# First layer's modulation vectors as column-tiled fp32 products, tokens loaded first, GpSimd's two-operand arithmetic on VectorE

## The chip, the core and the metric

One core of one Trainium2 chip runs the whole program. The time is device microseconds of one launch, the median of several runs. A core has TensorE (matmuls; PE in the rows, and PEld for its weight loads), VectorE (DVE), ScalarE (ACT), GpSimd (POOL) and SyncE (SP), whose queue issues the DMAs of this kernel.

## The reference, cut to what matters

Two layers work on 256 latent and 256 context tokens of 1024 channels. Each layer has a token-mixing part and a SwiGLU part, and each part is framed by norms that are modulated by six vectors made from the conditioning vector:

```python
silu_c = jax.nn.silu(c); silu_cc = jax.nn.silu(c_ctx)[None]
for l in range(DEPTH):                                   # DEPTH = 2
    mod_x = (silu_c @ w_ada[l] + b_ada[l]).reshape(B, 1, 6, D)
    mod_c = (silu_cc @ w_ada[l] + b_ada[l]).reshape(1, 1, 6, D)
    h = modulate(rms_norm(x, g_pre_mix[l]), mod_x[:, :, 0], mod_x[:, :, 1])
    hc = modulate(rms_norm(ctx, g_pre_mix[l]), mod_c[:, :, 0], mod_c[:, :, 1])
    ...   # p = h @ w_in[l]; attention, pooling and recurrent branch, gates, w_out -> mix_l
    x = x + mod_x[:, :, 2] * rms_norm(mix_l, g_post_mix[l])
    x = ffn_sublayer(x, mod_x[:, :, 3], mod_x[:, :, 4], mod_x[:, :, 5], ...)
    ...   # the same for ctx, in the first layer only
```

So each layer needs a shift, a scale and a gate (m = 0, 1, 2) for the mixing and three more (m = 3, 4, 5) for the SwiGLU part, for two streams in the first layer: w_ada[l] is 1024 x 6144, 25 MB a layer, read for two rows of products (one per stream).

## The kernel before, in words

All four token tiles of 128 (two of context, then two of latent tokens) stand in the moving operand, 512 columns. Weights are loaded as 512 KB pieces (`load_w`, line 605) and split into a high part (fp32r, a cast on ScalarE or VectorE) and a low part (a subtraction; `split_w`, line 614); activations are split likewise (`hilo`, line 640). Each product is then three fp32r matmuls: high x high, high x low, low x high (`mm3`, line 628). In the rows `whi`, `wlo` are the parts of weights, `hh`, `hl` those of the modulated tokens; `pm` and `pa` are the two sets of four PSUM banks.

Nothing is written to an engine directly. A `Queue` records every operation, and `Program.schedule` (line 256) is a list planner: it knows a price for each operation (`price`, line 207), the buffers, the PSUM banks and the port that VectorE and GpSimd share (`shares_port`, line 198), and hands the operations out in order of readiness and priority. An operation recorded through `either` or `also` may go to either of two engines, whichever is free first in the plan; so some of the two-operand subtractions (`wlo` above all) land on GpSimd. The order on each engine is fixed by that plan; on the chip the engines only wait for each other's semaphores. All records have one line, 409, so the rows are told apart by tiles.

**Start** (`start`, line 1177). The first layer's shift and scale are made on TensorE in eight blocks of 128 channels. A block is loaded as four DMAs of 256 KB (`start_load`), split into parts by casts and subtractions, and multiplied with the four columns of `cT` (high and low part of the two conditioning vectors): 16 fp32r matmuls of 256 columns a block. Two fp32 column pieces per block turn the rows back into columns. After every second block the tokens' transposes are modulated (`h_pair`, line 738) and multiplied with 512 columns of w_in (`products`), for the recurrent branch. The loads of the tokens stand between the first blocks' on SP's queue.

**Jobs.** All other modulation vectors are jobs that advance by one step at each `tick` (line 669), which the gemm loops call. A step loads 256 KB of w_ada into one of three `ra` buffers and VectorE multiplies it by a column of the silu and adds it to `acc`, 128 x 512 (`ada_acc`, line 651; one multiply-add per stream). After eight steps `ada_columns` (line 686) transposes `acc` on TensorE and sums it on VectorE into columns; `ada_gate` (line 700) sums it over the partitions with a `partition_all_reduce` on GpSimd and multiplies it by the post-norm's gain. The first layer's mixing runs the six jobs of m = 3, 4, 2; its SwiGLU part the job pairs of its own m = 5 and of all of the second layer's.

**Order of the stages**, in us of the profile: start to 68; the pooling, gate and q, k, v products to 190; recurrent chains, attention and the merges of the three branches to 395 (`rnn_chain`, `attention`, `merge`); output projection and norms to 510; SwiGLU to 815, norms to 861; the second layer's mixing to 1050, its norms to 1116, its SwiGLU to the end.

## Time and profile before

| | |
|---|---|
| median of 3 runs | 1312.26 us (1311.13 to 1313.22) |
| the profiled execution | 1311.86 us, span 1310.1 us, mean granted clock 0.984 |
| TensorE busy | 1238.5 us, 95% of the span |
| VectorE busy | 966.5 us, 74% |
| ScalarE busy | 631.1 us, 48% |
| GpSimd busy | 276.5 us, 21% |
| DMA | 199.5 MB, 152 GB/s over the span |

The span runs from the first instruction of the program to its last; the profiled time holds what lies around it as well. A busy TensorE counts the pipelined length of its matmuls, so what a matmul costs in a stream is the distance of two starts, which is shorter than the mean duration of a record. The granted clock is a share of the full 2.4 GHz.

### The profile page before, as it was taken

Reading aid. Unit: us, or ns where it says so; the run is one execution under the profiler, and the core shown is the slowest. Engines: PE = TensorE matmul, PEld = TensorE weight load, DVE = VectorE, ACT = ScalarE, POOL = GpSimd, SP = SyncE. Lnnn points to the kernel's source line nnn. Section 1 sums busy time; section 2 is a strip of 40 time slices with the busy share of each in tenths; the row PEclk is TensorE's granted clock in tenths of the full one; section 3 lists DMA queues with packets and bytes.
Section 4 is the critical chain, followed back from the end, with each engine's and each line's share of the span. In section 5 each row is a group of like instructions: output and inputs, shape, how many; then the busy total and the mean of one; then the engine's idle time right before and its main releaser. Section 6 shows DMA issues by size and latency. Waiting matters only on the chain.

```text
span 1310.1 us, 19123 instructions
## 1 busy us (share of the span) xinstructions
PE 1238.5 (95%) x7003; PEld 1067.9 (82%) x7003; DVE 966.5 (74%) x1552; ACT 631.1 (48%) x1173; POOL 276.5 (21%) x242
## 2 busy tenths in 40 slices
PE   6999998999999999999999999999888897999998
PEld 4888876777878887888888887799787796999986
DVE  5799989889788575688377731879998876555564
ACT  7736577477733373222122222666786744544400
POOL 4322023252541243010001004312333402000000
PEclk9999999999999999999999999999998999999999
DMA  9753523533238453656567831444344255566662
GB/s 292 241 143 91 160 89 107 166 114 89 60 97 265 154 173 90 200 171 199 177 210 225 251 114 62 137 118 141 113 129 130 81 168 166 149 179 191 181 193 78
DMA packets 249797, 199.53 MB, mean 152 GB/s; under 512 B 12724, under 2 KB 214740, under 8 KB 249704
## 3 DMA queue, kind: packets, MB, share of 16 engines
q1 hardware_dynamic: 249704, 198.32, 50.2%
q8 instruction: 55, 0.90, 0.3%
q14 instruction: 38, 0.31, 0.1%
HBM read 195.14 MB, written 3.15 MB: 151 GB/s over the span
## 4 chain that ended last, share of the span: by engine, by line
PE 77%; DVE 10%; ACT 5%; POOL 3%; issue 3%; DMA 1%; SPq 0%; DVEq 0%; POOLq 0%; ACTq 0%
PE pm L409 62%; PE pa L409 15%; DVE t L409 5%; ACT t L409 2%; POOL s L409 2%; DVE b L409 1%; DVE acc L409 1%; ACT junk_a L409 1%; DVE wlo L409 1%; POOL wlo L409 1%; ACT whi L409 1%; DVE s L409 1%; ACT b L409 1%; POOL b L409 0%; DMA raw<-in_w_in_dram 0%
## 5 line engine op out<-in xcount | busy, mean ns | idle before, releaser
L409 PE MATMUL pm<-hh,wlo 128*128 128x256 f32 (+1 forms) x1472 | 487.9, 333 | 9.9 <-DVE wlo L409 8.2
L409 PE MATMUL pm<-hl,whi 128*128 128x256 f32 (+1 forms) x1472 | 487.1, 332 | 3.4 <-DVE hl L409 3.4
L409 PE MATMUL pm<-hh,whi 128*128 128x256 f32 (+1 forms) x1472 | 485.3, 334 | 3.1 <-ACT hh L409 2.7
L409 ACT ACTIVATE whi<-raw 128x1024 fp32r<-128x1024 f32 (+1 forms) x225 | 229.4, 1026 | 265.6 <-PE pm L409 149.4
L409 DVE TENSOR_TENSOR wlo<-raw,whi 128x1024 fp32r<-128x1024 f32 (+1 forms) x212 | 254.2, 1202 | 96.7 <-ACT whi L409 92.7
L409 PEld LDWEIGHTS pm<-hh,wlo 128*128 128x128 f32 x1472 | 282.2, 192 | 37.2 <-DVE wlo L409 9.5
L409 PEld LDWEIGHTS pm<-hl,whi 128*128 128x128 f32 x1472 | 282.3, 192 | 29.1 <-DVE hl L409 4.5
L409 PEld LDWEIGHTS pm<-hh,whi 128*128 128x128 f32 x1472 | 280.0, 192 | 29.9 <-ACT hh L409 4.1
L409 POOL TENSOR_TENSOR wlo<-raw,whi 128x1024 fp32r<-128x1024 f32 (+1 forms) x58 | 142.3, 2458 | 316.9 <-ACT whi L409 143.4
L409 DVE SCALAR_TENSOR_TENSOR acc<-ra,csilu,acc 128x512 f32<-128x512 f32 x224 | 172.6, 795 | 28.2 <-DMA ra<-in_w_ada_dram 26.8
L409 PE MATMUL pm<-whi,b 128*128 128x512 f32 x360 | 140.7, 391 | 0.0
L409 PE MATMUL pa<-whi,b 128*128 128x512 f32 x360 | 140.4, 390 | 0.0
L409 PE MATMUL pm<-b,whi 128*128 128x512 f32 (+1 forms) x384 | 101.0, 344 | 13.6 <-ACT b L409 13.6
L409 ACT ACTIVATE tm<-pm 128x512 f32<-128x512 f32 (+1 forms) x92 | 44.7, 487 | 113.1 <-PE pm L409 112.8
L409 PEld LDWEIGHTS pm<-b,whi 128*128 128x128 f32 x384 | 66.7, 192 | 22.1 <-ACT b L409 14.4
L409 PEld LDWEIGHTS pm<-whi,b 128*128 128x128 f32 x360 | 67.6, 188 | 13.8
L409 PEld LDWEIGHTS pa<-whi,b 128*128 128x128 f32 x360 | 67.6, 188 | 13.8
L409 POOL PARTITION_ALL_REDUCE b<-acc x12 | 41.0, 3440 | 172.0 <-DVE acc L409 79.8
L409 PE MATMUL pm<-wlo,b 128*128 128x512 f32 x180 | 70.2, 390 | 3.1 <-DVE wlo L409 3.1
L409 POOL TENSOR_SCALAR s<-s 128x1 f32<-128x1 f32 x26 | 9.9, 382 | 298.1 <-ACT junk_a L409 297.6
L409 PE MATMUL pa<-wlo,b 128*128 128x512 f32 x180 | 70.4, 391 | 0.0
L409 PE MATMUL pm<-b,wlo 128*128 128x512 f32 (+1 forms) x192 | 65.5, 342 | 1.3 <-POOL wlo L409 1.3
(169 smaller groups left out, 1539.5 us busy)
## 6 DMA issues: line engine op xcount, KB each, us to landing
raw<-in_w_gu_dram SPq DMA_DIRECT2D x88, 512.0 KB
raw<-in_w_in_dram SPq DMA_DIRECT2D x84, 512.0 KB
ra<-in_w_ada_dram SPq DMA_DIRECT2D x160, 256.0 KB
raw<-in_w_down_dram SPq DMA_DIRECT2D x44, 512.0 KB
b<-in_w_ada_dram SPq DMA_DIRECT2D x32, 256.0 KB
raw<-in_w_out_dram SPq DMA_DIRECT2D x16, 512.0 KB
raw<-in_w_pool_o_dram SPq DMA_DIRECT2D x8, 512.0 KB
raw<-in_w_rnn_o_dram SPq DMA_DIRECT2D x8, 512.0 KB
```

Source lines behind the costliest of these rows:

```text
L409: op.fn(*op.args, **op.kw)
```

## The change

The modulation vectors of the first layer but for the SwiGLU gate are made by TensorE in full fp32, without a split. The two silu columns, padded with zeros to 32 columns (`cT`), are the weights. Eight blocks of 128 rows of w_ada are the moving operands, 512 columns each, and block k goes to the strip of 32 array columns k % 4 (`tile_position`), so that four sums of two blocks stand in four quarters of one bank. Four column pieces with a summing matrix turn it into columns (start and `row_columns`), or one product with a spread summing matrix broadcasts it to all partitions (`row_gate`), in place of transposes with reductions and of the all-reduce. In the start the four token tiles are loaded ahead of all modulation loads, four blocks of 256 channels (shift and scale) replace eight of 128, and all but the first of the `products` are 512 columns wide instead of two times 256. `either` is gone: the two-operand arithmetic that could go to either engine is VectorE's. The norms' small instructions, the all-reduces of the remaining gate jobs and the memsets stay on GpSimd. `ra` has eight buffers instead of three; a slot of the small working tiles shrinks from 640 to 576 columns; the padding tile moves and grows; the planner's DMA rate and the price of a tiled fp32 matmul are changed.

```diff
-SLOT = 640
+SLOT = 576
+BIAS = 2
...
-    c[:4, C_SUM:C_SUM + 2] = np.tile(np.eye(2, dtype=np.float32), (2, 1))
+    for j in range(4):
+        c[32 * j:32 * j + 2, C_SUM:C_SUM + 2] = np.eye(2, dtype=np.float32)
+    c[BIAS, C_SUM:C_SUM + 2] = 1.0
...
-    DMA_RATE = 360e3
+    DMA_RATE = 320e3
...
-                op.cost = max(n * 1.667e-3, 0.106)
+                op.cost = max(n * 1.667e-3 / (4 if "tile_position" in kw else 1), 0.106)
...
+    BUFS = {"raw": 4, "w": 10, "B": 30, "hT": 16, "t": 13, "s": 24, "ra": 8, "acc": 3, "hx": 3, "tm": 2}
...
-    PAD = 176
-    BUFS = {"raw": 4, "w": 10, "B": 30, "hT": 16, "t": 13, "s": 24, "ra": 3, "acc": 3, "hx": 3, "tm": 2}
+    PAD = 208
...
+        self.spread = self.const([128, 2, 128], F32, "spread")
+        nc.vector.tensor_copy(self.spread, self.c[:, C_SUM:C_SUM + 2].unsqueeze(2).to_broadcast([128, 2, 128]))
...
-        self.cT = self.const([128, 8, 4], F32R, "cT")
-        cst = cs.rearrange("p s k -> p k s")
-        nc.vector.tensor_copy(self.cT[:, :, 0:2], cst)
-        nc.vector.tensor_tensor(out=self.cT[:, :, 2:4], in0=cst, in1=self.cT[:, :, 0:2], op=ALU.subtract)
+        self.cT = self.const([128, 8, 32], F32, "cT")
+        nc.gpsimd.memset(self.cT, 0.0)
+        nc.vector.tensor_copy(self.cT[:, :, 0:2], cs.rearrange("p s k -> p k s"))
...
-        nc.either("tensor_tensor", out=lo[:, 0:n], in0=raw[:, 0:n], in1=hi[:, 0:n], op=ALU.subtract)
+        nc.vector.tensor_tensor(out=lo[:, 0:n], in0=raw[:, 0:n], in1=hi[:, 0:n], op=ALU.subtract)
...
-            r = nc.vector.tensor_tensor(out=lo, in0=src, in1=hi, op=ALU.subtract)
-            if src.tensor.name not in nc.psum:
-                nc.also(r, "gpsimd", "tensor_tensor", out=lo, in0=src, in1=hi, op=ALU.subtract)
+            nc.vector.tensor_tensor(out=lo, in0=src, in1=hi, op=ALU.subtract)
...
+    def ada_rows(self, l, m, h, done):
+        nc, w = self.nc, self.I["w_ada"][l]
+        c0 = m * D + h * 512
+        nc.sync.dma_start(out=self.brow[BIAS:BIAS + 1, :], in_=self.I["b_ada"][l:l + 1, c0:c0 + 512])
+        raws, landings = [], []
+        for k in range(8):
+            raws.append(self.sb("ra", [128, 512], F32, "ra"))
+            landings.append(nc.sync.dma_start(out=raws[k], in_=w[k * 128:(k + 1) * 128, c0:c0 + 512]))
+            if k < 7:
+                yield
+        ps = self.ps("pa")
+        for k in range(8):
+            j = k % 4
+            nc.after = landings
+            nc.tensor.matmul(ps[32 * j:32 * j + 32, :], lhsT=self.cT[:, k, :], rhs=raws[k], start=k < 4, stop=k >= 4,
+                             tile_position=(0, 32 * j))
+            nc.after = []
+        ar = self.sb("acc", [128, 512], F32, "acc")
+        nc.vector.tensor_tensor(out=ar, in0=ps, in1=self.brow, op=ALU.add)
+        done(ar)
+        yield
+    def row_columns(self, l, m, h, mods, g):
+        def done(ar):
+            nc = self.nc
+            dst = mods[m % 3][:, h * 4:(h + 1) * 4, :]
+            pc = self.ps("pa")
+            for i in range(4):
+                nc.tensor.matmul(pc[:, 2 * i:2 * i + 2], lhsT=ar[:, i * 128:(i + 1) * 128], rhs=self.c[:, C_SUM:C_SUM + 2],
+                                 start=True, stop=True)
+            p3 = pc[:, 0:8].rearrange("p (i s) -> p i s", s=2)
+            if m % 3 == 0:
+                nc.vector.tensor_copy(dst, p3)
+            else:
+                nc.vector.scalar_tensor_tensor(out=dst, in0=p3, scalar=1.0, in1=self.col(l, g, h * 4, 4).unsqueeze(2).to_broadcast([128, 4, 2]),
+                                               op0=ALU.add, op1=ALU.mult)
+        return self.ada_rows(l, m, h, done)
+    def row_gate(self, l, m, h, g_post, streams, ggs):
+        def done(ar):
+            nc = self.nc
+            gp = self.T(512)
+            nc.sync.dma_start(out=gp, in_=self.I[g_post][l, h * 512:(h + 1) * 512].partition_broadcast(128))
+            for s in streams:
+                ps = self.ps("pa")
+                nc.tensor.matmul(ps, lhsT=self.spread[:, s], rhs=ar, start=True, stop=True)
+                gg = self.B()
+                nc.vector.tensor_tensor(out=gg, in0=ps, in1=gp, op=ALU.mult)
+                ggs[s, h] = gg
+        return self.ada_rows(l, m, h, done)
...
-        blocks = [self.start_load(0)]
-        self.start_columns()
-        x = {t: self.load_x(t) for t in (0, 1)}
-        blocks.append(self.start_load(1))
-        hT, first = self.start(x, blocks)
+        hT, first = self.start()
+        x = {}
...
+    def start_load(self, c):
+        for k in range(8):
+            raw = self.B()
+            landing = self.nc.sync.dma_start(
+                out=raw.rearrange("p (m c) -> p m c", m=2),
+                in_=self.I["w_ada"][0][k * 128:(k + 1) * 128, 0:2 * D].rearrange("p (m c) -> p m c", m=2)[:, :, c * 256:(c + 1) * 256])
+            raws.append((raw, landing))
         return raws
...
+    def start_mods(self, c, raws, mt):
+        nc = self.nc
+        ps = self.ps("pa")
+        for k in range(8):
+            j = k % 4
+            nc.after = [landing for _, landing in raws[k - j:k - j + 4]]
+            nc.tensor.matmul(ps[32 * j:32 * j + 32, :], lhsT=self.cT[:, k, :], rhs=raws[k][0], start=k < 4, stop=k >= 4,
+                             tile_position=(0, 32 * j))
+            nc.after = []
+        ar = self.sb("tm", [128, TOK], F32, "tm")
+        nc.scalar.activation(ar, ps, AF.Copy)
+        pc = self.ps("pa")
+        for i in range(4):
+            nc.tensor.matmul(pc[:, 2 * i:2 * i + 2], lhsT=ar[:, i * 128:(i + 1) * 128], rhs=self.c[:, C_SUM:C_SUM + 2],
+                             start=True, stop=True)
+        for m in range(2):
+            nc.vector.tensor_tensor(out=mt[:, 2 * c:2 * c + 2, m], in0=pc[:, 4 * m:4 * m + 4].rearrange("p (k s) -> p k s", k=2),
+                                    in1=self.gcol[:, 16 + 8 * m + 2 * c:18 + 8 * m + 2 * c].unsqueeze(2).to_broadcast([128, 2, 2]),
+                                    op=ALU.add)
+        for k in (2 * c, 2 * c + 1):
+            nc.vector.tensor_scalar(out=mt[:, k, 1], in0=mt[:, k, 1], scalar1=1.0, scalar2=self.col(0, "g_pre_mix", k),
+                                    op0=ALU.add, op1=ALU.mult)
+    def start(self):
+        nc = self.nc
+        x = {t: self.load_x(t) for t in range(4)}
         mt = self.const([128, 8, 2, 2], F32, "mods0")
         mods = (mt[:, :, 0], mt[:, :, 1])
         hT = [None] * 8
         rx = [self.ps() for _ in range(4)]
+        raws = self.start_load(0)
+        self.start_columns()
+        xn = [self.pre_norm(x[t]) for t in range(4)]
...
+            parts = [slice(0, 256), slice(256, TOK)] if kp == 0 else [slice(0, TOK)]
+            for sl in parts:
...
+        ws = {}
+        for kp in range(5):
+            if kp < 4:
+                self.start_mods(kp, raws, mt)
+                raw = self.load_rx(kp)
+                if kp < 3:
+                    raws = self.start_load(kp + 1)
+                if kp == 2:
+                    self.load_rows()
+                    self.load_tables()
                 for s in range(2):
-                    self.h_pair(k // 2, s, [xn[2 * s], xn[2 * s + 1]], mods, hT)
-                if k > 1:
-                    products(k // 2 - 1, w)
-                w = self.split_w(raw)
-        products(3, w)
+                    self.h_pair(kp, s, xn[2 * s:2 * s + 2], mods, hT)
+                ws[kp] = self.split_w(raw)
+            if kp > 0:
+                products(kp - 1, ws.pop(kp - 1))
...
-                    self.jobs.append(self.ada_columns(0, m, h, streams, self.mods, "g_pre_ffn"))
+                    self.jobs.append(self.row_columns(0, m, h, self.mods, "g_pre_ffn"))
             for h in range(2):
-                self.jobs.append(self.ada_gate(0, 2, h, "g_post_mix", streams, self.ggs))
+                self.jobs.append(self.row_gate(0, 2, h, "g_post_mix", streams, self.ggs))
```

The remaining places of `nc.either("tensor_tensor", ...)` are replaced by `nc.vector.tensor_tensor(...)` in the same way: in the gate jobs, the recurrent chain (3), the pooling chain (2), the rotary part (2) and the attention's sink (2).

## Rows read from the trace of the kernel before

**Rows 1.** The page, part 1: busy us of each engine, share, instructions.

```profile
PE 1238.5 (95%) x7003; PEld 1067.9 (82%) x7003; DVE 966.5 (74%) x1552; ACT 631.1 (48%) x1173; POOL 276.5 (21%) x242
```

**Rows 2.** Windows by stage: length, busy us of PE, PEld, DVE, ACT, POOL, clock, DMA, GB/s.

```profile
0.00:68.00 68.00, 54.70 (x388) 44.29 (x389) 45.03 (x90) 49.25 (x101) 24.76 (x39) 0.97 0.85 261
68.00:190.00 122.00, 122.00 (x549) 100.71 (x548) 112.86 (x187) 66.56 (x100) 22.77 (x20) 1.00 0.42 125
190.00:395.00 205.00, 188.96 (x921) 150.84 (x920) 176.69 (x358) 127.89 (x290) 77.42 (x44) 0.98 0.36 106
395.00:510.00 115.00, 111.49 (x591) 94.90 (x590) 83.85 (x110) 52.13 (x96) 37.19 (x32) 1.00 0.60 185
815.00:861.00 46.00, 38.83 (x231) 33.48 (x230) 36.16 (x51) 26.59 (x61) 18.21 (x38) 1.00 0.38 121
900.00:1050.00 150.00, 131.24 (x946) 121.13 (x945) 132.17 (x253) 111.45 (x231) 52.29 (x32) 0.94 0.38 111
```

**Rows 3.** Timeline at 223 us: start, length, instruction, idle time before it and releaser.

```profile
223.12 2.82 POOL L409 TENSOR_TENSOR wlo<-raw,whi 128x1024 fp32r<-128x1024 f32 x1
...
223.64 2.86 DVE L409 TENSOR_TENSOR_SCAN t<-t,t,t 128x256 f32<-128x256 f32 x1
...
226.42 1.38 DVE L409 SCALAR_TENSOR_TENSOR acc<-ra,csilu,acc 128x512 f32<-128x512 f32 x2
227.72 1.21 DVE L409 TENSOR_TENSOR wlo<-raw,whi 128x1024 fp32r<-128x1024 f32 x1
...
228.99 0.79 PE L409 MATMUL pm<-hh,wlo 128*128 128x512 f32 x1 [4.08 <-DVE wlo L409]
```

**Rows 4.** Groups by form, whole span: count, busy us, mean ns, idle time before.

```profile
L409 DVE TENSOR_TENSOR wlo<-raw,whi 128x1024 fp32r<-128x1024 f32 x200 | 245.9, 1233 | 94.7 <-ACT whi L409 90.9 <-issue 0.9 <-PE pm L409 0.4
L409 DVE SCALAR_TENSOR_TENSOR acc<-ra,csilu,acc 128x512 f32<-128x512 f32 x224 | 172.6, 795 | 28.2 <-DMA ra<-in_w_ada_dram 26.8
...
L409 POOL TENSOR_TENSOR wlo<-raw,whi 128x1024 fp32r<-128x1024 f32 x52 | 133.1, 2566 | 305.6 <-ACT whi L409 136.3 <-PE pm L409 63.2 <-PE pa L409 42.1
...
L409 POOL PARTITION_ALL_REDUCE b<-acc x12 | 41.0, 3440 | 172.0 <-DVE acc L409 79.8 <-PE pa L409 76.7 <-issue 15.4
...
L409 PE MATMUL pa<-consts,tm 4*128 4x2 f32 x32 | 5.2, 264 | 2.3 <-ACT tm L409 2.1
```

**Rows 5.** Timeline of the start's later part: TensorE and ScalarE.

```profile
43.48 0.27 PE L409 MATMUL pa<-consts,t 128*128 128x128 f32 x1
...
44.39 0.82 PE L409 MATMUL pa<-consts,t 128*128 128x128 f32 x6
...
44.58 0.37 ACT L409 ACTIVATE tm<-pa 4x256 f32<-4x256 f32 x1 [0.49 <-PE pa L409]
...
47.08 0.41 ACT L409 ACTIVATE hh<-hx 128x256 fp32r<-128x256 f32 x1
...
67.89 0.40 PE L409 MATMUL pm<-hh,whi 128*128 128x512 f32 x1
```

**Rows 6.** Window of 5 us in the start, columns as in rows 2.

```profile
20.00:25.00 5.00, 4.19 (x26) 3.45 (x25) 4.74 (x10) 4.97 (x12) 0.80 (x2) 0.77 1.05 361
```

**Rows 7.** Chain that ended last, in order of time: start, length, what.

```profile
672.20 21.77 PE pm L409 x96
```

**Rows 8.** Window with the instructions on `acc` alone: PE, PEld, DVE, POOL, clock, DMA.

```profile
190.00:395.00 205.00, 2.07 (x16) 1.86 (x16) 48.85 (x57) 13.30 (x4) 0.98 0.36 106
```

**Rows 9.** Waits of SP's queue: us in total, times, longest.

```profile
SPq L409 <- DVE acc L409: 178.6, 123, 12.6
```

**Rows 10.** Waits of TensorE from 68 to 395 us: total, times, longest.

```profile
PE pm L409 <- DVE wlo L409: 8.0, 3, 4.1
```

**Rows 11.** Window with the instructions on `wlo` alone: PE, PEld, DVE, POOL, clock, DMA.

```profile
900.00:1050.00 150.00, 74.58 (x256) 49.50 (x255) 18.68 (x18) 43.72 (x18) 0.94 0.38 111
```

**Rows 12.** Chain that ended last near 496 us, columns as in rows 7.

```profile
496.27 3.31 POOL wlo L409
```

More of the change, by code (lines that the diff above doesn't have):

```diff
@@ L181, in record @@
         return op
-    def either(self, method, **kw):
-        op = getattr(self.vector, method)(**kw)
-        self.also(op, "gpsimd", method, **kw)
-        return op
     def also(self, which, eng, method, *args, **kw):
@@ L491, in load_constants @@
         self.c = self.const([128, C_W], F32, "consts")
+        if self.PAD:
+            self.const([128, self.PAD], F32, "pad")
         rows = self.const([112, 128], F32, "rows")
@@ L707, in done @@
                 nc.gpsimd.partition_all_reduce(gg, acc[s], channels=128, reduce_op=ReduceOp.add)
-                nc.either("tensor_tensor", out=gg, in0=gg, in1=gp, op=ALU.mult)
+                nc.vector.tensor_tensor(out=gg, in0=gg, in1=gp, op=ALU.mult)
                 ggs[s, h] = gg
@@ L864, in rnn_chain @@
             nc.after = []
-            nc.either("tensor_tensor", out=ti, in0=ti, in1=tr, op=ALU.mult)
+            nc.vector.tensor_tensor(out=ti, in0=ti, in1=tr, op=ALU.mult)
         yield
@@ L878, in rnn_chain @@
         hsum = hs[0][2][:, sl]
-        nc.either("tensor_tensor", out=hsum, in0=hsum, in1=hs[1][2][:, sl], op=ALU.add)
-        nc.either("tensor_tensor", out=hsum, in0=hsum, in1=gelu[ct][:, sl], op=ALU.mult)
+        nc.vector.tensor_tensor(out=hsum, in0=hsum, in1=hs[1][2][:, sl], op=ALU.add)
+        nc.vector.tensor_tensor(out=hsum, in0=hsum, in1=gelu[ct][:, sl], op=ALU.mult)
         ro = self.pair(full)
@@ L913, in pool_chain @@
             a0 = PADL + lo2
-            nc.either("tensor_tensor", out=nxt[:, :, a0:a0 + n], in0=cur[:, :, a0 - back:a0 - back + n],
+            nc.vector.tensor_tensor(out=nxt[:, :, a0:a0 + n], in0=cur[:, :, a0 - back:a0 - back + n],
                                     in1=cur[:, :, a0 + fwd:a0 + fwd + n], op=ALU.add)
@@ L920, in pool_chain @@
             ap = cur[:, :, PADL + e0:PADL + e0 + 8]
-            nc.either("tensor_tensor", out=ap, in0=ap, in1=self.c[:, c0:c0 + 8].unsqueeze(1).to_broadcast([128, ns, 8]), op=ALU.mult)
+            nc.vector.tensor_tensor(out=ap, in0=ap, in1=self.c[:, c0:c0 + 8].unsqueeze(1).to_broadcast([128, ns, 8]), op=ALU.mult)
         d = self.T(256 * ns)
@@ L949, in rope @@
         nc.vector.stream_shuffle(sw, x, [(i + 16) % 32 for i in range(32)])
-        nc.either("tensor_tensor", out=sw, in0=sw, in1=self.c[:, C_SIN:C_SIN + 256], op=ALU.mult)
-        nc.either("tensor_tensor", out=x, in0=x, in1=self.c[:, C_COS:C_COS + 256], op=ALU.mult)
+        nc.vector.tensor_tensor(out=sw, in0=sw, in1=self.c[:, C_SIN:C_SIN + 256], op=ALU.mult)
+        nc.vector.tensor_tensor(out=x, in0=x, in1=self.c[:, C_COS:C_COS + 256], op=ALU.mult)
         nc.vector.tensor_tensor(out=x, in0=x, in1=sw, op=ALU.add)
@@ L1016, in attn_scores @@
         es = self.small(2)
-        nc.either("tensor_tensor", out=es, in0=nm, in1=self.sink[:, h:h + 2], op=ALU.add)
+        nc.vector.tensor_tensor(out=es, in0=nm, in1=self.sink[:, h:h + 2], op=ALU.add)
         nc.scalar.activation(es, es, AF.Exp)
-        nc.either("tensor_tensor", out=es, in0=es, in1=rs, op=ALU.add)
+        nc.vector.tensor_tensor(out=es, in0=es, in1=rs, op=ALU.add)
         st["p"], st["den"] = pt, es
@@ L1164, in load_x @@
         return x
-    def start_load(self, k):
+    def start_load(self, c):
         raws = []
-        for q in range(2):
-            for m in range(2):
-                raw = self.B()
-                self.nc.sync.dma_start(
-                    out=raw.rearrange("p (k c) -> p k c", c=128),
-                    in_=self.I["w_ada"][0][q * 512:(q + 1) * 512, m * D + k * 128:m * D + (k + 1) * 128].rearrange("(k p) c -> p k c", p=128))
-                raws.append(raw)
-        return raws
-    def start(self, x, blocks):
-        nc, I = self.nc, self.I
-        xn = {}
+        for k in range(8):
[4 more added lines that the diff above has]
+            raws.append((raw, landing))
+        return raws
@@ L1183, in start @@
         rx = [self.ps() for _ in range(4)]
+        raws = self.start_load(0)
+        self.start_columns()
+        xn = [self.pre_norm(x[t]) for t in range(4)]
         def products(kp, w):
-            for s in range(2):
-                sl = slice(s * 256, (s + 1) * 256)
+            parts = [slice(0, 256), slice(256, TOK)] if kp == 0 else [slice(0, TOK)]
+            for sl in parts:
                 for kk in range(2):
@@ L1239, in start @@
-        products(3, w)
+                        self.mm3(rx[c][:, sl], (w[0][:, o:o + 128], w[1][:, o:o + 128]), h, kp + kk + sl.start == 0, kp == 3 and kk == 1)
+        ws = {}
[8 more added lines that the diff above has]
+                    self.load_tables()
+                for s in range(2):
+                    self.h_pair(kp, s, xn[2 * s:2 * s + 2], mods, hT)
+                ws[kp] = self.split_w(raw)
+            if kp > 0:
+                products(kp - 1, ws.pop(kp - 1))
```

48 lines of the change are left out of this document (4 added, 44 removed).

## The prediction

> **What bounds the kernel now.** I read the page's busy shares first: TensorE's share is 95%, VectorE's 74%, GpSimd's 21% [rows 1]. So the time is TensorE's work plus some 72 us in which it stands idle, and the next question is where those lie. The windows by stage tell it [rows 2]: the busy time taken from the length of each stage gives an idle time of 13.3 us in the start (0 to 68), none in 68 to 190, 16.0 in 190 to 395 (the recurrent and attention part of the first layer's mixing), 3.5 in 395 to 510, 7.2 in 815 to 861 and 18.8 in 900 to 1050 (the second layer's mixing). The rest is the norm chain near 1110 and the tail. In 190 to 395 VectorE is busy for 176.7 of 205 us, in 900 to 1050 for 132.2 of 150: there TensorE waits for VectorE. In 68 to 190 TensorE is full, so an instruction added to it there is paid in full, and one taken off VectorE gains nothing.
>
> How such a wait comes about stands in the timeline at 223 us [rows 3]. GpSimd subtracts a weight's high part for 2.82 us. A VectorE scan starts meanwhile and takes 2.86 us, ending only after GpSimd has ended. Two of the modulation multiply-adds (1.38 us) stand behind it, then the split that TensorE needs (1.21 us), and TensorE has been idle for 4.08 us. Both things that the change removes are in that chain.
>
> **The change part by part.**
>
> The unit price comes first: a group of eight full fp32 products, 32 columns wide, 512 long. No row shows one. The kernel's 16 column pieces in the start appear as 32 matmuls [rows 4], so each fp32 product is issued as two instructions. Six transposes at 44.39 take 0.82 us, a single one 0.27 [rows 5], so fp32 starts 0.11 us apart per 128 columns, or 0.43 us per 512 (estimate). Sixteen instructions one after the other would be 6.9 us; four strips quite side by side a quarter, 1.7 us. I take **2.2 us per group**, close to the lower end, because the four strips of a group share neither output rows nor columns of the array and each group waits until its loads have landed; the half microsecond is for the stagger. The range keeps 1.7 to 3.9. The Trainium skill, page TensorE: Matmul & The Clock Gate, Part 3, gives 2.38 times for three column strips side by side; by that a group would be 2.9 us (estimate) and the sum below some 6 us higher. No row here shows strips at all.
>
> Start. Gone are 128 split products, their casts on ScalarE and subtractions on VectorE and GpSimd; half of the column pieces go too. In come four groups. On SP's queue the eight token loads now stand ahead of the 32 modulation loads; the bytes stay. DMA moves 361 GB/s when it is full [rows 6]. With 2.1 MB of tokens and 2.1 MB for the first block, from some 3 us on at 330 GB/s, the first group can begin at 16 us. It runs at the lower clock (4.4 us); the chain behind it, from the copy out of the bank to the first high part, is 2.9 us before (44.58 to 47.49 [rows 5]) and I give it 4.5. So the first products start at 25 us. After that come four blocks of 24 products of 512 (0.227 each, from 96 in 21.77 us [rows 7]: 5.45 a block) and three times group, eight transposes and eight column pieces (2.2 + 0.9 + 1.0): 21.8 + 12.3. The end is at 59, and 60 with one stall. DMA needs 7.6 us a block (2.6 MB), less than TensorE's 9.5, so it stays covered; if it lost its rate, each block would wait. Before, the first 512-wide product of the next stage starts at 67.89 [rows 5]. **Gain 8 us.**
>
> First layer's shift, scale and gate. Six jobs leave VectorE: 96 multiply-adds of 0.795 us [rows 4], 76 us; the 48.9 us of accumulation in 190 to 395 [rows 8] are nearly all theirs. TensorE gets six groups (13.2 us) and four broadcasts of the gate, full fp32 products of 0.86 (3.4 us). The 16 new column pieces, 32 instructions of 0.11, replace 32 transposes of about the same, which is nothing. Six adds and four multiplies from the bank on VectorE replace eight reductions; four of twelve all-reduces of 3.4 us leave GpSimd [rows 4]. The sum on TensorE is **+16.6 us**, and as it is full or nearly so, I count all of it.
>
> SP's queue: its loads stood behind these accumulations for 178.6 us in all [rows 9]. With eight buffers instead of three a job's eight loads go out without it; what is late next is the job after it, which waits until the group has read its buffers, and the weight loads queued behind. TensorE's group waits for four landings in front of all products behind it; the tick spacing covers that, and without cover a landing costs 1 to 2 us each time.
>
> What comes back in 190 to 395: 16.0 us idle, and a granted clock of 0.98, which on 189 us is about another 3. VectorE loses 49 us of accumulation; GpSimd's work there comes to it at about half its length. Between all 19 and the 8.0 us that TensorE waits for VectorE's splits alone [rows 10] I take **-14 us**.
>
> GpSimd's two-operand work to VectorE. A split is 2.57 us on GpSimd and 1.23 on VectorE [rows 4]; but where the two overlap, VectorE stands as in [rows 3] for up to the whole GpSimd instruction. In 900 to 1050 18 GpSimd splits take 43.7 us [rows 11]; as VectorE work they are 22 us, and 22 us is about what it loses if each costs it 1.2. So I take VectorE's load as unchanged there, and the gain as latency alone: 3 us of 18.8. In 395 to 510 the split of 3.31 us at 496.27 [rows 12] ends on the chain and would take 1.2: 2 us. In 815 to 861 one multiply behind an all-reduce: 1 us. **Together -6 us**, with 0 to 10 for the range. The Trainium skill, page SBUF — State Buffer, section SBUF: two separate sides, says that the pair of ports is an exclusive lock, held for a whole instruction. The trace agrees: 2.86 us beside 2.82.
>
> The new prices in the planner, the buffer sizes and the padding add no work but reorder the program; I allow 3 us either way and count nothing.
>
> **Sum:** -8 + 16.6 - 14 - 6 = -11.4 us. The profiled execution took 1311.86 us around a span of 1310.1, 0.4 under the median of 1312.26; so 1300.5 of its kind, 1301 beside the median. A measurement can tell 0.2%, 2.6 us, from no change.
>
> **The rivals.**
>
> *The halves of a product keep each other waiting.* Each product is two instructions on one strip. If matmuls start in their order, the second half waits for the first and only neighbours overlap: nine steps of 0.43, 3.9 us a group. The first group falls in the wait for loads; the other three add 5 us to the start and six add 10 later: 1301 + 15 = **1316**. For it: the two instructions of the column pieces [rows 4]. Against it: nothing that a row shows. The same page's Part 3 says that matmuls are strictly first in, first out. Slower from 3.4 us a group on. Chance 0.25.
>
> *Strips don't overlap at all.* 6.9 us a group, nine times 4.7 more: **1343**. TensorE then pays in 68 to 190, where it has no idle time [rows 2]. Chance 0.12.
>
> *VectorE becomes the bound of the second layer.* There no accumulation leaves it, and it is idle for 17.8 of 150 us [rows 2]. If the waits on GpSimd were mostly spans of GpSimd's that nobody needed, 22 us of splits and some 4 of small subtractions come on top: 8 us more than fits, 11 worse than taken: **1312**, no change. Chance 0.1.
>
> That the change leaves GpSimd in the chains is partly so: eight all-reduces and the norms' small instructions stay, and their share is not in the sum.
>
> **How the numbers follow.** The forecast has 0.53, the rivals 0.25, 0.12 and 0.1. Below, 1.7 us a group (-4.5), all 19 us in 190 to 395 (-5) and 9 elsewhere (-3) give 1289. Above, the first rival with its 3 us of order and 3 of stalls gives 1322. What is left out is the second rival and tails. The forecast's own range is 1290 to 1309. Faster by over 0.2%: nearly all of the forecast, a fifth of the first rival, a third of the last: 0.6. Same 0.1, slower 0.3.
>
> **What would show it.** Right: the first 512-wide product of the next stage near 60 us; a group's matmuls ending within some 2.2 us of its first; 4 to 5 us idle on TensorE in the stage that was 190 to 395; no VectorE instruction twice its length beside a split. Wrong: starts within a group 0.43 us apart (first or second rival, by the ends), TensorE's busy time up by more than 15 us in all, or VectorE over 95% busy in the second layer's mixing.

## The result, and the profile after

The changed kernel takes **1288.41 us** (median of 4 runs, 1287.91 to 1290.7), beside 1312.74 us for the kernel before on the same chip: ratio 0.9828, 95% interval 0.9811 to 0.9844. I had said 1301, in a range of 1289 to 1322. The sign was right; the step down is 24 us where I worked out 11. The time is half a microsecond below the lower end of the range (0.9828 of the 1312.26 us that I had started from is 1289.7, just inside it). The profiled execution took 1287.92 us around a span of 1286.1.

The page of the changed kernel: busy times, and the shares of the chain that ended last.

```profile
PE 1235.7 (96%) x6971; PEld 1055.8 (82%) x6971; DVE 898.3 (70%) x1564; ACT 593.4 (46%) x1105; POOL 74.1 (6%) x129
...
PE 86%; DVE 5%; ACT 3%; issue 2%; POOL 2%; DMA 1%; SPq 0%; POOLq 0%; DVEq 0%; ACTq 0%
```

TensorE is nearly as busy as before (1238.5 [rows 1]): of the 24 us that the span lost, 21 are idle time. The windows of the changed kernel, over the stages that answer to [rows 2], with the same columns:

```profile
0.00:55.80 55.80, 43.88 (x252) 29.01 (x253) 23.59 (x66) 28.10 (x59) 6.00 (x31) 1.00 0.91 309
55.80:180.00 124.20, 124.20 (x573) 100.28 (x572) 92.62 (x169) 70.92 (x106) 2.16 (x6) 1.00 0.43 131
180.00:378.00 198.00, 196.43 (x1001) 154.17 (x1000) 161.57 (x375) 113.77 (x266) 0.00 (x0) 1.00 0.42 131
378.00:506.00 128.00, 116.01 (x611) 99.96 (x610) 82.53 (x116) 51.14 (x96) 26.70 (x28) 0.96 0.52 161
803.00:849.00 46.00, 44.13 (x265) 38.53 (x264) 31.33 (x55) 27.89 (x65) 14.58 (x36) 1.00 0.35 103
886.00:1028.00 142.00, 131.94 (x962) 121.88 (x961) 133.30 (x293) 110.94 (x228) 0.00 (x0) 0.98 0.41 118
```

Idle on TensorE (length less busy): 16.0 has become 1.6 in the recurrent part of the first layer, 18.8 has become 10.1 in the second layer's mixing. But 3.5 has become 12.0 in the stage of the output projection and its norms. That one got worse, which no step of my prediction said.

For the experiments I cut each profile at the same places: the first and last product with a branch's output weight (`pm<-b,wlo`) in either layer, and the first product of the SwiGLU and of the second layer. Lengths in us, each from the profiled execution:

| kernel | start, first products | first layer's merges | output projection, norms | SwiGLU, norms | second layer to its merges | its merges | rest |
|---|---|---|---|---|---|---|---|
| before | 159.8 | 258.0 | 45.9 | 378.4 | 84.1 | 157.2 | 226.7 |
| **changed** | 149.5 | 251.2 | 58.8 | 370.4 | 82.5 | 147.0 | 226.7 |
| b_no_gpsimd | 158.5 | 254.0 | 46.1 | 370.4 | 82.3 | 142.5 | 226.6 |
| b_idle_gpsimd | 156.6 | 256.1 | 46.1 | 370.3 | 93.3 | 159.2 | 227.0 |
| a_gpsimd_back | 151.1 | 252.7 | 60.4 | 380.6 | 84.2 | 156.7 | 227.7 |
| a_jobs_back | 149.5 | 255.4 | 58.9 | 370.9 | 82.5 | 147.2 | 226.1 |
| a_start_only | 150.1 | 260.3 | 60.0 | 380.9 | 84.2 | 157.0 | 226.9 |
| a_one_strip | 172.9 | 277.6 | 58.7 | 370.5 | 82.5 | 146.7 | 226.1 |
| a_mods_first | 153.9 | 251.2 | 59.0 | 370.8 | 82.5 | 146.8 | 226.2 |
| a_late_reduce | 149.7 | 251.2 | 45.6 | 379.4 | 82.5 | 148.3 | 226.6 |
| a_gate5_rows | 150.2 | 251.2 | 45.6 | 378.4 | 82.5 | 146.6 | 226.4 |
| a_gate5_mid | 149.7 | 251.1 | 45.7 | 370.6 | 82.5 | 147.1 | 226.8 |

So the change is -10.3 - 6.8 + 12.9 - 8.0 - 1.6 - 10.2 = -24.0 us by stage.

### The profile page after: what moved, and what is told of

The parts are those of the page before. It is cut to its first block, busy times and chain, and to the rows that moved or that the text cites. A ratio compares the mean times of both kernels' runs of the same rounds, so it can differ in the third digit from the quotient of the medians.

```text
span 1286.1 us, 18730 instructions
## 1 busy us (share of the span) xinstructions
PE 1235.7 (96%) x6971; PEld 1055.8 (82%) x6971; DVE 898.3 (70%) x1564; ACT 593.4 (46%) x1105; POOL 74.1 (6%) x129
## 4 chain that ended last, share of the span: by engine, by line
PE 86%; DVE 5%; ACT 3%; issue 2%; POOL 2%; DMA 1%; SPq 0%; POOLq 0%; DVEq 0%; ACTq 0%
PE pm L407 69%; PE pa L407 17%; DVE t L407 3%; ACT t L407 1%; POOL s L407 1%; DVE wlo L407 1%; DVE b L407 1%; DVE junk_v L407 1%; POOL b L407 1%; ACT junk_a L407 0%; ACT whi L407 0%; DMA b<-in_w_ada_dram 0%; DMA raw<-in_w_in_dram 0%; ACT hx L407 0%; DMA b<-in_ctx_dram 0%
## 5 line engine op out<-in xcount | busy, mean ns | idle before, releaser
L407 PE MATMUL pm<-hh,wlo 128*128 128x256 f32 (+1 forms) x1448 | 482.4, 335 | 5.9 <-DVE wlo L407 5.9
L407 PE MATMUL pm<-hl,whi 128*128 128x256 f32 (+1 forms) x1448 | 481.6, 334 | 0.3 <-DVE hl L407 0.3
L407 DVE TENSOR_TENSOR wlo<-raw,whi 128x1024 fp32r<-128x1024 f32 (+1 forms) x270 | 320.2, 1188 | 153.8 <-ACT whi L407 149.2
L407 ACT ACTIVATE whi<-raw 128x1024 fp32r<-128x1024 f32 (+1 forms) x219 | 223.2, 1024 | 274.0 <-PE pm L407 182.0
L407 PEld LDWEIGHTS pm<-hh,wlo 128*128 128x128 f32 x1448 | 276.1, 191 | 34.5 <-DVE wlo L407 6.9
L407 PEld LDWEIGHTS pm<-hl,whi 128*128 128x128 f32 x1448 | 276.1, 191 | 25.6 <-DVE hl L407 0.5
L407 DVE SCALAR_TENSOR_TENSOR acc<-ra,csilu,acc 128x512 f32<-128x512 f32 x140 | 101.3, 748 | 1.6
L407 PEld LDWEIGHTS pa<-whi,b 128*128 128x128 f32 x360 | 67.7, 188 | 13.7
L407 PE MATMUL pa<-consts,t 128*128 128x128 f32 x280 | 47.5, 296 | 26.6 <-DVE t L407 26.1
L407 PEld LDWEIGHTS pa<-consts,t 128*128 128x128 f32 x280 | 35.6, 152 | 37.3 <-DVE t L407 24.4
L407 POOL PARTITION_ALL_REDUCE b<-acc x8 | 26.5, 3326 | 631.0 <-DVE wlo L407 313.1
```

What stands on the lines that cost most here:

```text
L407: op.fn(*op.args, **op.kw)
```

## The experiments

### Which part does it: three parts taken back, one done alone

**b_no_gpsimd**: the kernel before, and nothing but GpSimd's two-operand arithmetic moved. The planner then orders all engines anew, so the new order may have a share in what comes out; b_idle_gpsimd, further down, keeps this order.

```diff
     def either(self, method, **kw):
-        op = getattr(self.vector, method)(**kw)
-        self.also(op, "gpsimd", method, **kw)
-        return op
+        return getattr(self.vector, method)(**kw)
...
-                    one, two = ("vector", "gpsimd") if m == 0 else ("gpsimd", "vector")
...
+                    nc.vector.tensor_tensor(out=lo[:, o], in0=raw, in1=hi[:, o], op=ALU.subtract)
```

The choice in `hilo` goes too.

> The kernel before with one part of the change alone: all two-operand arithmetic is VectorE's. Theory (GpSimd's instructions hold VectorE up for about as long as the work would take there, so VectorE's load stays and latency falls): 1303 to 1309. Rival (VectorE, with the jobs still on it, becomes the bound of the first layer's mixing): 1314 to 1325, with TensorE idle for over 20 us between 190 and 395.

Measured: 1285.91 us, ratio 0.9804 (0.9776 to 0.9833). That is 25 us, all that the whole change brings; both my numbers were wrong. (Its profiled execution lies at the lower end of its runs, 1282.21 to 1287.93, so its row in the table sums to a few us less.) Its busy times:

```profile
PE 1231.4 (96%) x7003; PEld 1065.4 (83%) x7003; DVE 968.1 (76%) x1672; ACT 632.0 (49%) x1165; POOL 88.1 (7%) x132
```

**a_gpsimd_back**: the changed kernel with `either` in its old places.

> The changed kernel with the two-operand work free to go to GpSimd again. Theory (my sum: latency behind slow GpSimd splits, mostly in the second layer's mixing and the norms): 3 to 10 us over 1288.4, so 1291 to 1299. Rival 1 (the whole surplus of the result over my forecast is GpSimd's): 1300 or more. Rival 2 (with VectorE emptied in the first layer the choice of the engine is worth nothing): 1286 to 1290.

Measured: 1315.69 us, ratio 1.0034 (1.0016 to 1.0053). The first rival holds: without this part, the change as a whole makes the kernel slower by 0.3%. GpSimd took only 28 weight splits there (before 52 [rows 4]), and the losses stand where they stood before: 10 us each in the SwiGLU with its norms and in the second layer's merges.

**a_jobs_back**: the changed kernel with the six jobs on VectorE, and with them four all-reduces on GpSimd.

```diff
-                    self.jobs.append(self.row_columns(0, m, h, self.mods, "g_pre_ffn"))
+                    self.jobs.append(self.ada_columns(0, m, h, streams, self.mods, "g_pre_ffn"))
...
-                self.jobs.append(self.row_gate(0, 2, h, "g_post_mix", streams, self.ggs))
+                self.jobs.append(self.ada_gate(0, 2, h, "g_post_mix", streams, self.ggs))
```

> The changed kernel with the six jobs of m = 2, 3, 4 back on VectorE, GpSimd still without two-operand arithmetic. VectorE gets 76 us of multiply-adds in the first layer's mixing, where it is now busy for 246 of 315 us; TensorE loses six groups and four broadcasts, some 10 us by the records. Theory (VectorE becomes the bound between 50 and 365 us): 10 to 20 us over 1288.4, so 1296 to 1308, with TensorE idle for 15 us or more there. Rival (the jobs fit into VectorE's free time once GpSimd no longer holds it up): 1279 to 1290.

Measured: 1292.74 us, ratio 0.9858 (0.9826 to 0.989): 4 us more than the changed kernel, short of the theory's 10 to 20 and above the rival. The first layer's merges, in the changed kernel and then in this one:

```profile
149.50:400.70 251.20, 249.63 (x1247) 196.97 (x1246) 199.28 (x427) 141.00 (x302) 0.00 (x0) 1.00 0.43 132
```

```profile
149.50:404.90 255.40, 242.42 (x1158) 195.78 (x1157) 232.85 (x482) 153.05 (x319) 13.42 (x4) 0.97 0.40 122
```

VectorE is busy for 232.9 of 255 us and TensorE idle for 13.0 instead of 1.6; against that TensorE is busy for 7.2 us less, although the granted clock is 0.97 instead of 1.00. The jobs' move is a small gain: the intervals of the two ratios overlap, and the 4.2 us are this stage's.

**a_start_only**: the edits of a_gpsimd_back and a_jobs_back together, so that the new start, the buffers and the planner's prices are left.

> The changed kernel with the six jobs of the first layer back on VectorE and the two-operand work free to go to GpSimd again: what is left of the change is the start, the buffers and the planner's prices. Theory (the start alone is worth what its trace shows, the first 512-wide product of the next stage at 50.4 us for 67.9): 1312.7 - 17.5, so 1293 to 1298 us. Rival (my sum: 8 us in the start, and the rest of the surplus came from the other two parts): 1302 to 1307. Second rival (the gain in the start is lost again at the loads behind it): 1309 or more.

Measured: 1322.63 us, ratio 1.0091 (1.0064 to 1.0118). By the number that is the second rival's, but not by its cause: the start does gain 9.7 us by the table; the output projection with its norms loses 14.1, the SwiGLU 2.5, the first layer's merges 2.3. Of the 14.1, 11.55 are one stall of TensorE, until 466.26, behind an all-reduce on GpSimd and not behind loads; the changed kernel has it too (below). So the stage that got worse comes with the new start, buffers and prices, whatever the jobs and GpSimd do.

### Why GpSimd's arithmetic cost so much

**b_idle_gpsimd**: b_no_gpsimd, and 25 subtractions on GpSimd that nobody needs, put in behind the finished plan, so that every engine runs the same instructions in the same order.

```diff
+            if self.nsplit % 2 == 0 and n == 1024:
+                nc.extra[op.idx] = dict(out=self.idle, in0=hi, in1=hi, op=ALU.subtract)
...
                 op.fn(*op.args, **op.kw)
+                if op.idx in self.extra:
+                    self.gpsimd.engine.tensor_tensor(**self.extra[op.idx])
```

> The kernel before with all two-operand arithmetic on VectorE (0.980 of the time before), and 25 subtractions of 128 x 1024 put on GpSimd in the second layer's mixing, one behind every second weight's high part. They write a tile that nothing reads, and the order of every other engine is the same to the instruction. Theory 1 (what GpSimd's instructions cost is that they hold VectorE up while they run, whoever needs their result): 8 to 14 us come back in the second layer's mixing and nowhere else, so 1294 to 1300 us, with VectorE instructions of two to three times their length beside them and TensorE stalls of 4 us or more. Theory 2 (the cost was latency: TensorE waited for a split of 2.57 us in place of 1.23): nobody waits for these, so 1284 to 1288.

Measured: 1310.65 us, ratio 1.0002 (0.9987 to 1.0017). The whole gain of b_no_gpsimd is gone again, about twice what theory 1 asked, and by the table in the second layer's mixing (93.3 for 82.3 and 159.2 for 142.5; the other stages differ by 2 us at most). Nothing reads these results, so GpSimd's instructions can cost as much without anyone waiting for what they make. That does not say that latency had no share in the kernel before. The windows of those two stages, first without the 25 instructions, then with them:

```profile
829.00:911.30 82.30, 80.39 (x605) 76.72 (x604) 71.79 (x141) 56.98 (x112) 9.58 (x19) 1.00 0.43 125
911.30:1053.80 142.50, 135.36 (x1046) 127.67 (x1045) 128.79 (x272) 105.54 (x215) 0.00 (x0) 0.99 0.48 139
```

```profile
829.10:922.40 93.30, 84.73 (x606) 79.52 (x606) 81.18 (x143) 57.99 (x113) 33.13 (x32) 0.96 0.38 109
922.40:1081.60 159.20, 140.68 (x1045) 131.24 (x1044) 151.61 (x273) 104.34 (x214) 36.85 (x17) 0.95 0.41 122
```

VectorE is busy for 232.8 instead of 200.6 us. Of the 27.7 us that the two stages grow, TensorE is idle for 18.0 (252.5 - 225.4 against 224.8 - 215.8) and busy for 9.7 more: the granted clock falls to 0.96 and 0.95 of full speed, with part of the time at the lower of its two levels, and its matmuls last longer. How one such hold looks, in the timeline of this kernel:

```profile
936.48 2.91 DVE L407 TENSOR_TENSOR_SCAN t<-b,t 128x512 f32<-128x512 f32 x3
...
940.25 2.04 POOL L409 TENSOR_TENSOR idle<-whi 128x1024 fp32r<-128x1024 f32 x1 [6.06 <-ACT whi L407]
940.53 2.84 DVE L407 TENSOR_TENSOR wlo<-raw,whi 128x1024 fp32r<-128x1024 f32 x1
...
943.43 0.58 PE L407 MATMUL pm<-b,wlo 128*128 128x256 f32 x1 [2.47 <-DVE wlo L407]
...
975.96 2.23 POOL L409 TENSOR_TENSOR idle<-whi 128x1024 fp32r<-128x1024 f32 x1 [4.15 <-ACT whi L407]
976.69 4.28 DVE L407 TENSOR_TENSOR_SCAN t<-b,t 128x512 f32<-128x512 f32 x3
```

A split of 1.23 us [rows 4] lasts 2.84, and ends 1.1 us after GpSimd has ended; TensorE waits for it. Three scans take 4.28 us; three of the same form take 2.91 at 936.48, beside no GpSimd instruction.

Three more lines of this kernel show that VectorE's being held is not all:

```profile
839.92 1.89 POOL L409 TENSOR_TENSOR idle<-whi 128x1024 fp32r<-128x1024 f32 x1
...
842.35 1.41 DVE L407 SCALAR_TENSOR_TENSOR b<-t,s,b 128x512 f32<-128x512 f32 x2 [2.44 <-POOL s L407]
...
879.89 6.83 POOL L409 TENSOR_TENSOR idle<-whi 128x1024 fp32r<-128x1024 f32 x1
```

At 839.92 the subtraction stands on GpSimd's own queue ahead of a norm's small instruction, for which VectorE waits 2.44 us, and TensorE behind it 2.16 (until 846.53), where b_no_gpsimd has 0.72 and 0.44: of the 18.0 us of idle time, 1.7 come this way. And at 879.89 it is GpSimd that is held: it takes 6.83 us while VectorE's instructions beside it keep their usual lengths. The kernel before has the hold at the place of its longest stall (6.52 us on TensorE until 985.84):

```profile
978.89 5.19 POOL L409 TENSOR_TENSOR wlo<-raw,whi 128x1024 fp32r<-128x1024 f32 x2 [0.18 <-ACT whi L409]
979.18 2.77 DVE L409 TENSOR_TENSOR_SCAN t<-b,t 128x256 f32<-128x256 f32 x1
981.87 2.49 DVE L409 TENSOR_TENSOR t<-t,t 128x256 f32<-128x256 f32 x1
...
985.84 0.80 PE L409 MATMUL pm<-b,whi 128*128 128x256 f32 x2 [6.52 <-ACT b L409]
```

Two splits run back to back on GpSimd. A scan of 256 columns, 0.67 us in the changed kernel, takes 2.77, and the multiply behind it 2.49: each waits for one whole GpSimd instruction. The end of that chain, a copy on ScalarE, is what TensorE waits for. The Trainium skill, page SBUF — State Buffer, section SBUF: two separate sides, says the same: whoever starts first has the port pair for its whole instruction and the other is fully blocked; the 2.84 beside 2.04 agree.

### What the strips are worth

**a_one_strip**: all eight products of a group on one strip; what reads the sums then reads 32 rows. The jobs' groups, shown here, and the start's alike:

```diff
-            nc.tensor.matmul(ps[32 * j:32 * j + 32, :], lhsT=self.cT[:, k, :], rhs=raws[k], start=k < 4, stop=k >= 4,
-                             tile_position=(0, 32 * j))
+            nc.tensor.matmul(ps[0:32, :], lhsT=self.cT[:, k, :], rhs=raws[k], start=k == 0, stop=k == 7,
+                             tile_position=(0, 0))
```

> The changed kernel with all eight products of a group on one strip of 32 columns, one sum after the other, in the same order on every engine. Theory (the strips run side by side): an instruction starts 0.4 us or more behind the one before, a group takes 6 to 7 us in place of 1.1; three groups of the start that are exposed and six later add 5.5 each, some 50 us, less what was idle: 1325 to 1340. Rival (a product of 32 columns is cheap by itself, the strips do nothing): 1286 to 1292.

Measured: 1336.74 us, ratio 1.0196 (1.017 to 1.0222), as the theory has it. One group of the jobs in the timeline, first of the changed kernel, then of this one (start, duration of the 16 instructions together):

```profile
160.02 1.92 PE L407 MATMUL pa<-ra,cT 128*32 128x512 f32 x16
```

```profile
183.41 7.05 PE L407 MATMUL pa<-ra,cT 128*32 128x512 f32 x16
```

1.92 us against 7.05: four strips side by side give 3.7 times. Ten groups of 5.1 us make 51; the runs are 48 apart.

### Where the start's gain went

In the changed kernel TensorE stands idle for 11.69 us until 456.77. The timeline there:

```profile
443.33 3.60 POOL L407 PARTITION_ALL_REDUCE b<-acc  x1 [5.76 <-PE pa L407]
...
453.92 0.45 POOL L407 TENSOR_SCALAR s<-s 128x1 f32<-128x1 f32 x2 [6.98 <-issue]
...
455.56 0.75 DVE L407 SCALAR_TENSOR_TENSOR b<-t,s,b 128x512 f32<-128x512 f32 x1 [9.66 <-POOL s L407]
...
456.77 1.54 PE L407 MATMUL pa<-consts,t 128*128 128x128 f32 x6 [11.69 <-DVE t L407]
```

The norm's small instruction at 453.92 needs the sums of squares, which ScalarE has by 446.7 at the latest. But on GpSimd's queue an all-reduce of the SwiGLU gate stands ahead of it, and behind that come 6.98 us in which GpSimd does nothing that the profile shows. The all-reduce itself had started 5.76 us after the last instruction before it. (The profile names TensorE as what ended that; in after_again, below, the same distance is 5.9 us and ended by nothing that shows.) So one all-reduce between two small instructions keeps them 16 us apart.

**a_late_reduce**: the all-reduces ordered behind the norms' last small instruction.

```diff
+                nc.after = [self.last_rstd] if (l, m) == (0, 5) else []
                 nc.gpsimd.partition_all_reduce(gg, acc[s], channels=128, reduce_op=ReduceOp.add)
+                nc.after = []
...
+        self.last_rstd = nc.gpsimd.tensor_tensor(out=r, in0=a[:, 1:2], in1=self.mhalf, op=ALU.pow)
```

> The changed kernel with one order more: the four all-reduces of the first layer's SwiGLU gate are planned behind the last of the norms' small GpSimd instructions of the same layer. Theory (the 11.7 us in which TensorE is idle at 457 us are GpSimd's: the all-reduce and 7 us of nothing behind it stand ahead of the norm's reciprocal root): the stall falls to some 1 us, 1276 to 1280. Rival (the norm there is late for another reason, VectorE or the token loads, and the all-reduce is only in its company): 1286 to 1290.

Measured: 1284.54 us, ratio 0.9798 (0.9776 to 0.9821). The stage falls from 58.8 to 45.6 us as the theory said, but the SwiGLU behind it grows from 370.4 to 379.4, so the sum is between theory and rival. Its timeline shows a cost that I had not listed:

```profile
464.39 9.81 POOL L407 PARTITION_ALL_REDUCE b<-acc  x3 [6.93 <-issue]
467.68 2.76 DVE L407 TENSOR_TENSOR b<-b,t 128x512 f32<-128x512 f32 x1 [5.82 <-POOL b L407]
470.36 3.13 DVE L407 TENSOR_TENSOR hl<-hx,hh 128x256 fp32r<-128x256 f32 x3
...
470.82 0.58 PE L407 MATMUL pm<-hl,whi 128*128 128x256 f32 x1 [4.99 <-DVE hl L407]
...
473.41 0.68 DVE L407 TENSOR_TENSOR b<-b,t 128x512 f32<-128x512 f32 x1
```

An all-reduce holds VectorE as a subtraction does: the multiply takes 2.76 us beside the second of the three and 0.68 later. The tokens' low parts (`hl`) wait behind, and TensorE for them.

**a_gate5_rows**: the same gate on the array (`row_gate(0, 5, ...)` for `ada_gate(0, 5, ...)`).

> The changed kernel with the first layer's SwiGLU gate made on TensorE like the mixing's gate: two more groups (1.1 us each) and four broadcasts, some 4 us of TensorE in a stage in which it is full; four of the eight all-reduces and 32 multiply-adds on VectorE are gone, so no all-reduce stands near the norms at 457 us. Theory: 11 us of stall gone, 4 paid, 1279 to 1283. Rival (the stall stays, the norm waits for something else): 1291 to 1295.

Measured: 1283.34 us, ratio 0.9789 (0.9766 to 0.9812). That is 0.3 us above the theory's range. The stall is gone (45.6); the SwiGLU, where TensorE is full, pays 8.0 for two groups and four broadcasts, twice what I had put down.

**a_gate5_mid**: the gate's jobs moved in the list, nothing else.

```diff
-            for h in range(2):
-                self.jobs.append(self.ada_gate(0, 5, h, "g_post_ffn", streams, ggs))
             for m in (0, 1):
...
+            for h in range(2):
+                self.jobs.append(self.ada_gate(0, 5, h, "g_post_ffn", streams, ggs))
             for h in range(2):
                 self.jobs.append(self.ada_gate(1, 2, h, "g_post_mix", [1], self.next_ggs))
```

> The changed kernel with the two jobs of the first layer's SwiGLU gate behind the eight column jobs of the second layer instead of ahead of them: its four all-reduces then stand in the middle of the SwiGLU, in one row with the other gates', and no GpSimd instruction of a norm stands behind one. Theory (the all-reduce costs TensorE nothing by itself, only where a norm's small instructions or its VectorE instructions are near): output projection and norms fall from 58.8 to 46 us, the SwiGLU stays at 370, 1274 to 1278. Rival (the stall moves on, as it did to the start of the SwiGLU when the reduce came right behind the norms): 1283 to 1289.

Measured: **1275.62 us**, ratio 0.9729 (0.9716 to 0.9743), as the theory says. The window of the output projection and norms, in the changed kernel and then in this one:

```profile
378.00:490.00 112.00, 100.01 (x540) 86.72 (x539) 67.23 (x96) 47.33 (x91) 26.70 (x28) 0.95 0.49 150
```

```profile
378.00:490.00 112.00, 111.16 (x597) 96.04 (x596) 60.24 (x86) 50.97 (x96) 11.40 (x24) 1.00 0.47 146
```

Idle falls from 12.0 to 0.8 us, and the granted clock is 1.00 instead of 0.95. This version beats both kernels. **after_again** ran beside it:

> The changed kernel itself, beside the version with the moved gate jobs on the same chip: 0.981 to 0.984 of the kernel before, so 1286 to 1291.

Measured: 1287.98 us, ratio 0.9822 (0.9809 to 0.9835). So moving two lines is worth 12.4 us, half as much as the whole change.

### Tokens first

**a_mods_first**: `raws = self.start_load(0)` ahead of the token loads.

> The changed kernel with the first block of modulation loads ahead of the tokens' loads again. Theory (the norm of the tokens is the longer chain behind the loads, so tokens belong first): the first product of the start moves from 22.1 us to 25 or 27, 1290 to 1294. Rival (the bytes are the same and both are needed, so the order does nothing): 1287 to 1290.

Measured: 1292.7 us, ratio 0.9858 (0.9844 to 0.9871). The time is the theory's, the way to it isn't: the first product starts at 22.67 instead of 22.10 us, and yet the start ends 4.4 us later. The first 25 us, of the changed kernel and then of this one:

```profile
0.00:25.00 25.00, 13.08 (x68) 6.49 (x72) 8.65 (x24) 12.32 (x28) 5.85 (x29) 1.00 0.94 322
```

```profile
0.00:25.00 25.00, 14.29 (x44) 6.17 (x44) 8.61 (x25) 11.57 (x27) 6.23 (x29) 0.82 0.90 308
```

The granted clock is 0.82 instead of 1.00 there. TensorE has done 44 matmuls instead of 68, and the two halves of the second group start at 25.10 and 29.44 us instead of 20.09 and 24.84. Whether the clock or the order of the loads decides was not taken apart.

## Why the prediction was right in sign and too small

**The unit price held.** I took 2.2 us for a group, in 1.7 to 3.9; it is 1.92. The first rival (halves that wait, 3.9) and the second (no overlap, 6.9) are out: 6.9 is what one strip costs (7.05). By the rule of the Trainium skill, page TensorE: Matmul & The Clock Gate, Part 3, that I weighed (2.38 times for three strips), a group would have been 2.9 us (estimate); four strips measure 3.7 times.

**The start was too small, and not by the group.** I gave it 8 us, from 67.89 [rows 5] to 60. The start has 120 products, and the next one begins at 55.76:

```profile
11.50 4.54 PE L407 MATMUL pa<-b,cT 128*32 128x512 f32 x10 [0.46 <-DMA b<-in_w_ada_dram]
...
22.10 0.74 PE L407 MATMUL pm<-hh,whi 128*128 128x256 f32 x4 [0.79 <-ACT hh L407]
...
24.84 1.07 PE L407 MATMUL pa<-b,cT 128*32 128x512 f32 x8
...
55.76 0.39 PE L407 MATMUL pm<-hh,whi 128*128 128x512 f32 x1
```

The first group begins as its loads land, at 11.50, where I let it wait for the last of them until 16; so products start at 22.1 for 25. From there to the end it is 33.7 us, which I had at 35. Gain 12.1, of which 10.3 is left at the first merge.

**The jobs' work on TensorE was about what I said, and more came back.** I set +16.6 against -14. In the changed kernel the six groups and the four broadcasts are busy for 15.3 us:

```profile
L407 PE MATMUL pa<-ra,cT 128*32 128x512 f32 x96 | 11.5, 599 | 0.0
...
L407 PE MATMUL pa<-acc,spread 128*128 128x512 f32 x8 | 3.8, 602 | 0.0
```

The 32 instructions of the new column pieces take 3.9 us, the 32 transposes that go 4.4: nothing, as I said. Idle in the recurrent stage fell by 14.4 us, as I said too; but some 11 of that belong to the jobs (13.0 in a_jobs_back), and some 3 come with GpSimd's part alone (12.6 in b_no_gpsimd, where the jobs are on VectorE). Yet TensorE's busy time is only 7.5 us higher than with the jobs on VectorE (1235.7 against 1228.2). In a_jobs_back the granted clock in the merges is 0.97, which is 13.7 us of the stage at the lower of the two levels, so its matmuls last longer; here it is 1.00. For the clock I had some 3 us. So the move is worth some -4 us (1292.74 against 1288.41) where my sum had +2.6.

**The step that failed is GpSimd's.** I wrote: "So I take VectorE's load as unchanged there, and the gain as latency alone: 3 us of 18.8", and -6 in all, 0 to 10. It is -25 alone (b_no_gpsimd) and -27 as the last part (a_gpsimd_back). The load was indeed unchanged: VectorE is busy for 966.5 us before [rows 1] and 968.1 in b_no_gpsimd. But an engine's load says nothing of where it is held. I had the hold in [rows 3], 2.86 us beside 2.82, and booked it as load, to be set off against the 22 us of splits; its price is paid by the short instructions of a chain at whose end TensorE waits, a scan or a multiply of 0.4 to 0.7 us that lasts 2.5 to 2.8. The 25 idle subtractions show that this can cost as much as the whole part brought. Nor did I count that the stalls bring the clock down: a third of b_idle_gpsimd's loss is longer matmuls.

In 395 to 510 and 815 to 861 I gave this part 3 us. The SwiGLU stage with its norms alone returned 8.0. There the two longest stalls come from GpSimd's queue and not from the hold, in the kernel before:

```profile
485.62 3.31 POOL L409 PARTITION_ALL_REDUCE b<-acc  x1 [7.99 <-DVE acc L409]
496.27 3.30 POOL L409 TENSOR_TENSOR wlo<-raw,whi 128x1024 fp32r<-128x1024 f32 x1 [7.33 <-issue]
...
499.62 0.50 PE L409 MATMUL pm<-hh,wlo 128*128 128x512 f32 x1 [1.75 <-POOL wlo L409]
...
811.41 6.49 POOL L409 PARTITION_ALL_REDUCE b<-acc  x2 [7.76 <-issue]
...
819.82 0.50 PE L409 MATMUL pm<-wlo,b 128*128 128x512 f32 x1 [3.14 <-DVE wlo L409]
```

The split on GpSimd stood behind an all-reduce: from the reduce's end at 488.9 to the split's start at 496.27 [rows 12] are 7.3 us of GpSimd's silence, and 7.4 from 791.5 to 798.89, which I read past. At 819.82 TensorE waits for a split that stands on VectorE behind two all-reduces, and these begin 7.76 us after GpSimd's last split. How much of the 25 us is the hold and how much this silence was not taken apart for the kernel before. And the multiply behind an all-reduce, for which I set 1 us in 815 to 861, no run shows: GpSimd's only two-operand instruction on whole tiles there is a split at 841.62, and the multiply, at 814.70, is VectorE's.

**A term was missing.** I wrote that eight all-reduces stay "and their share is not in the sum". Their share is +12.9 us in the stage of the output projection: the new order puts one of them ahead of a norm. a_gate5_mid takes the term out with an edit of its place alone. That the total still came out at the edge of my range is luck in part: this term and GpSimd's, some 19 us too small, are errors in opposite directions.

**The third rival** (VectorE becomes the bound of the second layer) had no ground: VectorE is as busy there as before (130.5 of 147 against 131.8 of 157) and TensorE waits less.

What stays open: the changed kernel's second-layer merges are 4.5 us longer than b_no_gpsimd's, with a stall of 4.37 us at 989.87 in which the split that TensorE needs stands behind small attention instructions on VectorE. It is in every kernel with the new start and without GpSimd's arithmetic, and I did not take apart which of the buffers and prices orders it so. Nor was the clock's part separated from the order of the loads in a_mods_first.

## What to carry to other kernels

Before work is moved to GpSimd, look at what VectorE does meanwhile: beside a two-operand instruction or an all-reduce there, a VectorE instruction can stand until GpSimd has ended (2.84 us for 1.23), and what counts is not the sum of both loads but whether a short VectorE instruction on a chain to TensorE stands beside it. An all-reduce belongs in a stretch where neither the norms nor the chains of activations are near, and next to other all-reduces. And a saving at one end of a planned program is only worth what the orders behind it leave: compare stage by stage, the loss may be a single queue entry.

## What the runs showed of the hardware that I had not expected

- 25 GpSimd subtractions of 2.54 us whose result nobody reads cost 25 us of a kernel in which VectorE has a quarter of its time free: 63 us of GpSimd's work and 32 us of VectorE's busy time became 25 us of the program's time.
- Between an all-reduce and a different GpSimd instruction lie 5.8 and 6.4 us ahead of it (443.33 and 475.67 in the changed kernel) and 7.0 behind it (453.92), in which GpSimd shows nothing. In all kept traces together, 41 changes in each direction, none is shorter than 5.76 us ahead and 6.71 behind; two all-reduces in a row can follow each other at once (793.11 in the changed kernel). The Trainium skill, page GPSIMD Engine Reference, section 2.1 Instruction dispatch, states some 6 us for the first call of freshly loaded code, without a visible instruction. The distances ahead are of that size; that code is loaded there is not shown.
- Four column strips in full fp32 run 3.7 times as fast as one, two instructions per product and all: 16 instructions in 1.92 us.
